# Two solves start later, unit 4's key loads get a pause, group norm's transposes go in pairs, and layer B's roundings are spread behind casts

## The chip, the core and the metric

The kernel runs on one core of a Trainium2 chip. The metric is device time in microseconds (us) of one execution. The core has five engines with a queue of instructions each: TensorE (PE, with its weight loads as PEld), VectorE (DVE), ScalarE (ACT), GpSimd (POOL) and SyncE (SP), whose queue here issues nearly all DMAs. Each engine takes its instructions strictly in order. An instruction that waits for a semaphore holds up everything behind it on its engine.

## The reference

The program is one inference step of a two-layer decoder for a prompt of 272 tokens (16 of them meta tokens) and 8 samples of one token, 280 columns in all. Layer A is RWKV-7 time mixing, layer B sliding-window attention with sinks.

```
for layer A (width D = 2048, 64 heads of 64):
    xm = x + (shifted x - x) * mu                      # six mixes
    r, k, v, z = xm[0..3] @ w_rkvz                      # four products, 2048 x 4096 each
    decay, a  = two small LoRA products
    kk = k * k_k ;  kk = kk / max(|kk| per head, 1e-12)  # the key norms
    k  = k * (1 + (a - 1) * k_a) ;  b = kk * a
    S_t = S * d - (S kk) b + v k ;   y_t = S_t r         # a scan over 272 tokens per head
    y  = group_norm(y) + (sum r k r_k) v ;  h += (y * silu(z)) @ w_out
shared k, v = rmsnorm(h) @ w_kv
for layer B:  q, z = rmsnorm(h) @ w_qz ; h += (attention(q, k, v) * silu(z)) @ w_o
final rmsnorm
```

Outputs are y for prompt and samples, the final states S, the shift rows and the two caches, all in float32.

## The kernel before, in words

**Products.** Every float32 weight matrix is multiplied in three passes of a reduced-precision type. `split` (L192) makes of a raw weight tile `raw` a rounded half `whi` (a cast on ACT, L195) and the rest `wlo` (a subtraction on DVE, L197). `mm3` (L216) then issues three products: `whi` times the rounded activations, `whi` times their rest, `wlo` times the rounded ones (L218 to L220). A weight tile of 128x512 (256 KB) is called a unit of weights here. The pools hold five of each of `raw`, `whi` and `wlo`, so that a cast can run at most some units ahead of PE.

**Pieces.** In layer A the order of PE's work is written out by hand. `products` (L709) goes through the large products (r, k, v, z, then a part of the output product `o`), and yields after each piece: six matmuls of 128x280. One product of 256 columns is 16 pieces, and one unit of weights serves two of them. `drive` (L610) counts the pieces in `self.pos` and lets the other streams add their own small PE work between them. A stream yields a number of pieces after which it is to be called again, and sometimes a condition. `mark` and `after` (L636, L639) are such conditions.

**The streams.** The 64 heads are 16 units of four heads (numbers 0 to 15 in names such as `kk4`; not the units of weights), and eight pairs of units (0 to 7).

- `prep` (L858) makes each unit ready: it loads k and r, and spreads the key norms over the partitions with two DMAs (`spread`, L560). It multiplies k by them into `kk` (L898, DVE). Behind that stand the rest of the inputs: two scans on DVE (L910), exponentials on ACT (L916 to L918), six POOL copies (L932), transposes on PE. The key norms of units 4 to 7 come out of `key_norms` (L552): a DMA from a DRAM tensor `kr`, a reciprocal root on DVE, and a DMA back.
- `scores`, `substitute` and `solve` (L984, L1053, L1089) build and invert a triangular matrix for each pair. `substitute` is a long run of small DVE instructions on `NL`, at whose end two DVE transposes give `TN` (L1081) and `TR` (L1082). From `TR` four ACT instructions make `TT` (L1085, 3.13 us). `solve` begins a fixed number of pieces after the scores. Its first PE work (L1102) reads `TN`, and then DVE, ACT and PE take turns (L1104, L1108, L1112, L1115, L1120, L1124, L1129, L1132).
- `chain` (L1155) runs the scan over time for a pair in five chunks.
- `group_norm` (L1256) normalises the chain's result Y, waits 36 pieces, transposes it on PE in four groups of three 128x128 transposes (L1275), three pieces apart, and adds each to the unit's bonus tile `vT` on DVE (L1276). Two groups share a PSUM tile of two banks, of which the pool has only one. The chains use the same pool. The unit's `yd` store follows (L1279).
- `decode` does the same for the samples on DVE.

**What sets DVE's, ACT's and SP's order.** The scheduler of the framework puts the instructions of the other engines in order, by its own estimates of time. Hand-set bounds on it are `high_priority` and `issue_after`, which keeps an instruction behind another one in this order. In `drive` most streams' work stands behind a late weight split (`self.los[-2]`, L621).

**Into layer B.** `out_a` (L1423) ends layer A. `phase_b` (L1469) computes k and v with four products of `w_kv`, eight units of weights each. Layer B's normalised inputs `bmh`, `bml` are made by `norm_mix` (L1459), 16 times: one ACT instruction (L1464) for the rounded half and one on DVE (L1465) for the rest. They are read later, by the q product.

Of the kernel before, what the change touches and what calls it, by code (L numbers as in the profile page):

```python
# [25 lines left out]
L = NM + SEQ  # L26
# [4 lines left out]
KT = D // 128  # L31
# [4 lines left out]
NU = NP // 2  # L36
GZ = 12
# [22 lines left out]
P_AN, P_MU, P_KVN, P_BN = 0, 16, 112, 128  # L60
# [49 lines left out]
class Kernel:  # L110
    def __init__(self, nc, tc, I, O):
        self.nc, self.tc, self.I, self.O = nc, tc, I, O

        self.raws, self.los = [], []

        self.wx = self.hold = None
        self.behind = []
        self.plan = []
        self.pools = {}
# [72 lines left out]
    def split(self, hi, lo, src):  # L192

        with self.tc.issue_after(self.root) if self.hold else contextlib.nullcontext():
            self.nc.scalar.copy(hi, src)  # L195
        with self.tc.issue_after(self.hold) if self.hold else contextlib.nullcontext():
            return self.nc.vector.tensor_tensor(lo, src, hi.bitcast(F32), op=ALU.subtract)  # L197

    def wunits(self, w, name, nk, col, nc_, per):

        nc = self.nc
        assert nc_ == 256 and per == 2, (nc_, per)
        for k0 in range(0, nk, per):
# [7 lines left out]
            self.raws.append(nc.sync.dma_start(raw.rearrange("p k c -> p (k c)"), w[col // 256, k0 // 2]))  # L211
            hi, lo = t("whi", F32R), t("wlo", F32R)
            self.los.append(self.split(hi, lo, raw))
            yield k0, hi, lo

    def mm3(self, ps, wh, wl, xh, xl, start, stop):  # L216
# [641 lines left out]
    def prep(self, u):  # L858
# [35 lines left out]

        kk = w("kk")
        self.spread(kk, self.kr[u // 4][4 * u % 16:4 * u % 16 + 4])
        for j in range(2):
            V.scalar_tensor_tensor(kk[:, j], kT[:, j], self.pcol(P_KK, p0 + j), kk[:, j], op0=MU, op1=MU)  # L898

# [189 lines left out]
    def solve(self, o):  # L1089
# [4 lines left out]
        ev = lambda n, *s: rp.tile([128, 512], F32, tag="ev", bufs=2, name=f"{n}{o}")[:, :s[0] * s[1]].rearrange(  # L1094
            "p (i t) -> p i t", t=s[1])

        yield 24 if o < 5 else 27
        ps = self.bank(self.pe, f"ps_so{o}")
        Q = [slice(32 * q, 32 * q + 32) for q in range(4)]
        for i in range(16):  # L1100
# [155 lines left out]
    def group_norm(self, o):  # L1256

        nc, rp = self.nc, self.rp
        V, A = nc.vector, nc.scalar
        MU, AD = ALU.mult, ALU.add  # L1260
        Y, var = self.Y, self.gvar
        y = Y.rearrange("p c j q i -> p (c j q) i")
        bc = lambda a: a.unsqueeze(2).to_broadcast((128, 24, 64))
        V.tensor_scalar(var, var, 1.0 / 64, GN_EPS, op0=MU, op1=AD)
        self.rsqrt(var, rp, "y", o)
        V.tensor_tensor(y, y, bc(var), op=MU)
        for j in range(4):
            u = 2 * o + j // 2
            b = self.U[u]['bonus']
            yield 3 if j else 36 if o < NU // 2 - 1 else 19  # L1270
            if j % 2 == 0:
                two = self.two_banks(f"ps_yt{o}_{j}")
            ps = two[:, j % 2]
            for c in range(3):
                nc.tensor.transpose(ps[:, 128 * c:128 * c + 128], Y[:, c, j].rearrange("p q i -> p (q i)"), self.ident)  # L1275
            V.scalar_tensor_tensor(b[:, j % 2, :L], ps[:, :L], self.pcol(P_GG, 4 * o + j), b[:, j % 2, :L],  # L1276
                                   op0=MU, op1=AD)
            if j % 2 and o < GZ // 2:
                nc.sync.dma_start(self.yd[u // 2][:, 2 * (u % 2):2 * (u % 2) + 2, :L], b[:, :, :L])  # L1279
        self.mark('g', o)  # L1280

# [141 lines left out]
    def out_a(self):  # L1423
# [11 lines left out]
        for k in range(KT):  # L1435
# [15 lines left out]
            if k >= KT - 2:  # L1451
                nc.tensor.matmul(pst[:, :N], ones, acc if k == KT - 2 else sq, start=k == KT - 2,
                                 stop=k == KT - 1)
        units = self.wunits(self.I['w_kv'][0], "kv", KT, 0, 256, 2)
        self.kvu = itertools.chain([next(units) for _ in range(5)], units)
        nc.scalar.activation(self.rb, pst[:, :N], AF.Ln, bias=self.epst, scale=1.0 / D)
# [12 lines left out]
    def phase_b(self):  # L1469
# [18 lines left out]
        with self.tc.tile_pool(name="kvm", bufs=2, reuse_waits="tile") as pool:  # L1488
# [44 lines left out]
            dma(f('p_cache_v')[0], self.Vd)  # L1533
            dma(f('s_cache_k')[:, WIN - 1], ksn)
            dma(O['s_cache_v'][:, WIN - 1], self.Vn[0:64:8, :, 0])
            self.bmx = [self.norm_mix(bp, "bm", P_BN, k) for k in range(KT)]
        self.wx = None
        self.close("wx0", "st0", "kv")
        right = dict(side="right", reuse_waits="tile")
# [433 lines left out]
```

## Time and profile before

| | |
|---|---|
| median of 3 runs | 2120.92 us (2119.35 to 2124.57) |
| the profiled execution | 2118.32 us |
| its span, first to last instruction | 2116.5 us |
| PE busy | 2064.9 us (98%) |
| DVE busy | 1697.8 us (80%) |
| ACT busy | 1263.8 us (60%) |
| mean granted TensorE clock | 0.99 |

The profiled execution has 1.8 us outside its span and lies 2.6 us under the median of the three runs. In timelines each row gives the start in us from the span's start, the duration, engine, line, operation, tiles, shape, count, and in brackets the engine's idle time before the row with what ended it. Matmuls overlap: a row's duration is not its spacing, which the next row's start gives. A granted clock of 0.50 means that TensorE ran at half speed in that stretch.

### The profile page before, as it was taken

The page shows a single profiled execution, that of the slowest core. Times are in us where ns is not written, and L with a number is a line of the kernel's source. Part 1 is how long each engine was busy: PE and PEld are TensorE (multiplying, and loading weights), DVE is VectorE, ACT ScalarE, POOL GpSimd, SP SyncE. Part 2 cuts the span into 40 slices and gives each one's busy share as a digit, 9 for nine tenths or more (in the row PEclk, how much of TensorE's full clock was granted, in tenths as well). Part 3 has the DMA queues.
Part 4 walks back from the last instruction along what each step waited for, and adds up shares of the span by engine and source line. Part 5 has one row for each costly group of instructions (what it writes and reads, how often), then busy time and mean ns, then how long its engine had stood idle before and what let it go on. Part 6 is the DMA issues. An engine that isn't in the chain of part 4 may idle for free.

```text
span 2116.5 us, 55871 instructions
## 1 busy us (share of the span) xinstructions
PE 2064.9 (98%) x21420; PEld 1965.8 (93%) x21420; DVE 1697.8 (80%) x4112; ACT 1263.8 (60%) x2790; POOL 122.5 (6%) x188
## 2 busy tenths in 40 slices
PE   9999999899999999999999999999999999999997
PEld 7999899889899989899999999999999999999997
DVE  8867777687678878888888788997888888878885
ACT  3457766576766757767676445565565655544443
POOL 0011100001010010100100001100000000000000
PEclk9999999999999999999999999999999999999999
DMA  7898667658756876777657687757455444567774
GB/s 258 314 312 250 189 213 241 188 181 290 216 180 205 260 229 198 211 217 222 203 152 246 207 257 243 247 172 227 132 167 156 146 155 130 181 210 247 232 219 132
DMA packets 276356, 446.28 MB, mean 211 GB/s; under 512 B 54056, under 2 KB 97768, under 8 KB 275696
## 3 DMA queue, kind: packets, MB, share of 16 engines
q1 hardware_dynamic: 275656, 441.66, 66.6%
q8 instruction: 168, 2.75, 0.5%
q10 hardware_dynamic: 432, 1.05, 0.1%
q14 instruction: 100, 0.82, 0.1%
HBM read 381.69 MB, written 65.03 MB: 211 GB/s over the span
## 4 chain that ended last, share of the span: by engine, by line
PE 87%; DVE 5%; ACT 3%; DMA 3%; issue 2%; SPq 0%; POOL 0%; DVEq 0%; POOLq 0%; ACTq 0%
PE ps_z L218 6%; PE ps_z L219 6%; PE ps_z L220 6%; PE ps_k L218 3%; PE ps_ob L218 3%; PE ps_ob L220 3%; PE ps_v L218 3%; PE ps_ob L219 3%; PE ps_r L218 3%; PE ps_q L218 3%; PE ps_q L220 3%; PE ps_q L219 3%; PE ps_k L219 3%; PE ps_k L220 3%; PE ps_v L220 3%; PE ps_v L219 3%
## 5 line engine op out<-in xcount | busy, mean ns | idle before, releaser
L218 PE MATMUL ps_z<-mhlm,whi_z 128*128 128x280 f32 x512 | 158.6, 310 | 2.8 <-ACT sr L937 2.0
L219 PE MATMUL ps_z<-mhlm,whi_z 128*128 128x280 f32 x512 | 150.6, 294 | 0.0
L220 PE MATMUL ps_z<-mhlm,wlo_z 128*128 128x280 f32 x512 | 150.3, 294 | 0.0
L218 PE MATMUL ps_q<-bmh,whi_qb 128*128 128x264 f32 x512 | 150.0, 293 | 0.1
L218 PE MATMUL ps_z<-bmh,whi_zb 128*128 128x264 f32 x512 | 147.4, 288 | 0.0
L220 PE MATMUL ps_q<-bmh,wlo_qb 128*128 128x264 f32 x512 | 145.6, 284 | 0.6 <-DVE wlo_qb L197 0.6
L219 PE MATMUL ps_q<-bml,whi_qb 128*128 128x264 f32 x512 | 145.6, 284 | 0.0
L219 PE MATMUL ps_z<-bml,whi_zb 128*128 128x264 f32 x512 | 145.5, 284 | 0.0
L220 PE MATMUL ps_z<-bmh,wlo_zb 128*128 128x264 f32 x512 | 145.4, 284 | 0.0
L218 PE MATMUL ps_ob<-ghi,whi_ob 128*128 128x264 f32 x512 | 145.3, 285 | 0.0
L220 PE MATMUL ps_ob<-ghi,wlo_ob 128*128 128x264 f32 x512 | 144.6, 284 | 0.0
L219 PE MATMUL ps_ob<-glo,whi_ob 128*128 128x264 f32 x512 | 144.6, 283 | 0.0
L195 ACT CAST whi_ob<-raw_ob 128x512 fp32r<-128x512 f32 x128 | 79.1, 620 | 96.9 <-PE ps_ob L219 77.8
L195 ACT CAST whi_oa<-raw_oa 128x512 fp32r<-128x512 f32 x128 | 79.2, 620 | 88.0 <-PE ps_oa L219 30.6
L197 DVE TENSOR_TENSOR wlo_r<-raw_r,whi_r 128x512 fp32r<-128x512 f32 x128 | 87.8, 691 | 42.6 <-ACT whi_r L195 41.3
L218 PE MATMUL ps_v<-mhlm,whi_v 128*128 128x280 f32 x384 | 119.8, 312 | 0.4 <-ACT st L790 0.4
L218 PE MATMUL ps_k<-mhlm,whi_k 128*128 128x280 f32 x384 | 119.1, 310 | 1.0 <-ACT st L790 1.0
L195 ACT CAST whi_v<-raw_v 128x512 fp32r<-128x512 f32 x128 | 79.0, 619 | 65.8 <-PE ps_v L219 37.7
L197 DVE TENSOR_TENSOR wlo_v<-raw_v,whi_v 128x512 fp32r<-128x512 f32 x128 | 87.3, 687 | 36.9 <-ACT whi_v L195 35.6
L195 ACT CAST whi_zb<-raw_zb 128x512 fp32r<-128x512 f32 x128 | 78.2, 619 | 62.9 <-PE ps_z L219 38.5
L220 PE MATMUL ps_k<-mhlm,wlo_k 128*128 128x280 f32 x384 | 112.4, 293 | 2.1 <-issue 2.1
L219 PE MATMUL ps_v<-mhlm,whi_v 128*128 128x280 f32 x384 | 112.7, 293 | 0.0
(478 smaller groups left out, 7604.1 us busy)
## 6 DMA issues: line engine op xcount, KB each, us to landing
raw_k<-a_w_rkvz SPq DMA_DIRECT2D x128, 256.0 KB
raw_v<-a_w_rkvz SPq DMA_DIRECT2D x128, 256.0 KB
raw_r<-a_w_rkvz SPq DMA_DIRECT2D x128, 256.0 KB
raw_z<-a_w_rkvz SPq DMA_DIRECT2D x128, 256.0 KB
raw_oa<-a_w_out SPq DMA_DIRECT2D x128, 256.0 KB
raw_qb<-b_w_qz SPq DMA_DIRECT2D x128, 256.0 KB
raw_zb<-b_w_qz SPq DMA_DIRECT2D x128, 256.0 KB
raw_ob<-b_w_o SPq DMA_DIRECT2D x128, 256.0 KB
```

The costliest lines, as they stand in the source:

```text
L195: self.nc.scalar.copy(hi, src)
L197: return self.nc.vector.tensor_tensor(lo, src, hi.bitcast(F32), op=ALU.subtract)
L218: mm(ps, wh, xh, start=start, stop=False)
L219: mm(ps, wh, xl, start=False, stop=False)
L220: return mm(ps, wl, xh, start=False, stop=stop)
```

## The change

Four places of the source change.

1. In `prep`, unit 4 alone: after the DMAs that spread its key norms, the stream yields 7 pieces before `kk` is made of them.
2. In `solve`, the number of pieces between the scores and the first PE work is 29 instead of 24 for pair 1, and 31 instead of 27 for pair 6. The other six keep theirs.
3. In `group_norm`, the four groups of three transposes become two of six, six pieces apart. Both DVE instructions of a unit follow the six transposes. The second store, and the mark that chains and later units wait for, then come 42 pieces after the start, where they came after 45.
4. In `phase_b`, the 16 calls of `norm_mix` for layer B each stand behind one cast of `w_kv`'s units: the first behind the eighth cast (unit of weights 7), the last behind the 23rd.

No operation of arithmetic is added or taken away, and the number of matmuls is the same.

```diff
@@ split, wunits: remember the cast
-            self.nc.scalar.copy(hi, src)
+            self.cast = self.nc.scalar.copy(hi, src)
...
             self.los.append(self.split(hi, lo, raw))
+            self.casts.append(self.cast)
@@ prep
         kk = w("kk")
         self.spread(kk, self.kr[u // 4][4 * u % 16:4 * u % 16 + 4])
+        if u == 4:
+            yield 7
         for j in range(2):
             V.scalar_tensor_tensor(kk[:, j], kT[:, j], self.pcol(P_KK, p0 + j), kk[:, j], op0=MU, op1=MU)
@@ solve
-        yield 24 if o < 5 else 27
+        yield (24, 29, 24, 24, 24, 27, 31, 27)[o]
@@ group_norm
-        for j in range(4):
-            u = 2 * o + j // 2
+        for i in range(2):
+            u = 2 * o + i
             b = self.U[u]['bonus']
-            yield 3 if j else 36 if o < NU // 2 - 1 else 19
-            if j % 2 == 0:
-                two = self.two_banks(f"ps_yt{o}_{j}")
-            ps = two[:, j % 2]
-            for c in range(3):
-                nc.tensor.transpose(ps[:, 128 * c:128 * c + 128], Y[:, c, j].rearrange("p q i -> p (q i)"), self.ident)
-            V.scalar_tensor_tensor(b[:, j % 2, :L], ps[:, :L], self.pcol(P_GG, 4 * o + j), b[:, j % 2, :L],
-                                   op0=MU, op1=AD)
-            if j % 2 and o < GZ // 2:
+            yield 6 if i else 36 if o < NU // 2 - 1 else 19
+            two = self.two_banks(f"ps_yt{o}_{i}")
+            for k in range(2):
+                for c in range(3):
+                    nc.tensor.transpose(two[:, k, 128 * c:128 * c + 128], Y[:, c, 2 * i + k].rearrange("p q i -> p (q i)"),
+                                        self.ident)
+            for k in range(2):
+                V.scalar_tensor_tensor(b[:, k, :L], two[:, k, :L], self.pcol(P_GG, 4 * o + 2 * i + k), b[:, k, :L],
+                                       op0=MU, op1=AD)
+            if o < GZ // 2:
                 nc.sync.dma_start(self.yd[u // 2][:, 2 * (u % 2):2 * (u % 2) + 2, :L], b[:, :, :L])
@@ out_a
+        self.kv0 = len(self.casts)
         units = self.wunits(self.I['w_kv'][0], "kv", KT, 0, 256, 2)
@@ phase_b
-            self.bmx = [self.norm_mix(bp, "bm", P_BN, k) for k in range(KT)]
+            self.bmx = []
+            for k in range(KT):
+                with self.tc.issue_after(self.casts[self.kv0 + 7 + k].ins):
+                    self.bmx.append(self.norm_mix(bp, "bm", P_BN, k))
```

The scheduler reacts to all of this, and from pair 1 on the order of DVE, ACT, POOL and SP differs in many places. Three of them follow. Line numbers of the changed source are 1 to 5 higher than those of the kernel before. The last number in a name is a serial number.

The first place is DVE while the key norms of unit 4 come in, before. `stmp1_14` and the row behind it on `NL1` are the last step of pair 1's substitution, `wlo_v_1280_12` is a weight split, `vT0` a bonus tile of pair 0's group norm.

```order
L197 TENSOR_TENSOR wlo_v_1280_12_5407<-raw_v_1280_12_5404,whi_v_1280_12_5406 128x512
L898 SCALAR_TENSOR_TENSOR kk4_5449<-kT4_5445,par_79,kk4_5449 128x280
L1075 TENSOR_TENSOR stmp1_14_5118<-NL1_5077 128x28
L898 SCALAR_TENSOR_TENSOR kk4_5449<-kT4_5445,par_79,kk4_5449 128x280
L910 SCALAR_TENSOR_TENSOR cl4_4871<-reset_1751,cl4_4871 128x272 x2
L904 TENSOR_TENSOR kT4_5445<-kT4_5445,km0_4_5454 128x280
L1077 TENSOR_TENSOR NL1_5077<-NL1_5077,stmp1_14_5118 128x2x14
L197 TENSOR_TENSOR wlo_v_1280_14_5425<-raw_v_1280_14_5422,whi_v_1280_14_5424 128x512
L904 TENSOR_TENSOR kT4_5445<-kT4_5445,km1_4_5457 128x280
L906 TENSOR_TENSOR ta4_4872<-ta4_4872,kk4_5449 128x560
L1081 STREAM_TRANSPOSE TN1_5123<-NL1_5077 128x512
L1082 STREAM_TRANSPOSE TR1_5124<-NL1_5077 128x512
```

The same place now:

```order
L197 TENSOR_TENSOR wlo_v_1280_12_5412<-raw_v_1280_12_5409,whi_v_1280_12_5411 128x512
L1078 TENSOR_TENSOR stmp1_14_5118<-NL1_5077 128x28
L1080 TENSOR_TENSOR NL1_5077<-NL1_5077,stmp1_14_5118 128x2x14
L1084 STREAM_TRANSPOSE TN1_5123<-NL1_5077 128x512
L1085 STREAM_TRANSPOSE TR1_5124<-NL1_5077 128x512
L197 TENSOR_TENSOR wlo_v_1280_14_5430<-raw_v_1280_14_5427,whi_v_1280_14_5429 128x512
L1280 SCALAR_TENSOR_TENSOR vT0_2043<-ps_yt0_0_5399,par_79,vT0_2043 128x272 x2
L197 TENSOR_TENSOR wlo_v_1536_0_5455<-raw_v_1536_0_5452,whi_v_1536_0_5454 128x512
L197 TENSOR_TENSOR wlo_v_1536_2_5483<-raw_v_1536_2_5480,whi_v_1536_2_5482 128x512
L197 TENSOR_TENSOR wlo_v_1536_4_5508<-raw_v_1536_4_5505,whi_v_1536_4_5507 128x512
L901 SCALAR_TENSOR_TENSOR kk4_5449<-kT4_5445,par_79,kk4_5449 128x280 x2
```

The two multiplications into `kk4` have moved from the place right behind `wlo_v_1280_12` to one behind four more weight splits, and `TN1`, `TR1` and group norm's two additions into `vT0` now stand ahead of them.

The second place is DVE where `TN5` is made, which the solve of pair 5 reads on PE. Before:

```order
L197 TENSOR_TENSOR wlo_z_768_0_14541<-raw_z_768_0_14538,whi_z_768_0_14540 128x512
L1075 TENSOR_TENSOR stmp5_14_13987<-NL5_13946 128x28
L197 TENSOR_TENSOR wlo_z_768_2_14629<-raw_z_768_2_14626,whi_z_768_2_14628 128x512
L1077 TENSOR_TENSOR NL5_13946<-NL5_13946,stmp5_14_13987 128x2x14
L1081 STREAM_TRANSPOSE TN5_13992<-NL5_13946 128x512
L1082 STREAM_TRANSPOSE TR5_13993<-NL5_13946 128x512
```

Now:

```order
L197 TENSOR_TENSOR wlo_z_512_6_14356<-raw_z_512_6_14353,whi_z_512_6_14355 128x512
L1078 TENSOR_TENSOR stmp5_14_13925<-NL5_13884 128x28
L1280 SCALAR_TENSOR_TENSOR vT9_10726<-ps_yt4_1_14291,par_79,vT9_10726 128x272 x2
L1080 TENSOR_TENSOR NL5_13884<-NL5_13884,stmp5_14_13925 128x2x14
L795 SCALAR_TENSOR_TENSOR st3_2_14313<-th2_0_14315,st3_2_14313 128x280
L1084 STREAM_TRANSPOSE TN5_13930<-NL5_13884 128x512
```

`TN5` stood behind the split of `z_768_2`, whose first matmul is piece 786 of PE's order, while the solve's first PE work (L1102) stood at piece 778: eight pieces apart. Now it stands behind `z_512_6`, first used at piece 774, with the solve at piece 772: two apart. Pair 5's own number of pieces has not changed.

The third place is ACT at the start of the `w_kv` products. Before (nine roundings `bmh0` to `bmh8` stand just ahead of these rows, behind the cast of `kv_0_12`):

```order
L1457 ACT_TABLE_LOAD
L1457 ACTIVATE rb_20527<-rb_20527 128x280
L1464 ACTIVATE bmh9_22753<-hT_20526,par_79 128x280
L1464 ACTIVATE bmh10_22757<-hT_20526,par_79 128x280
L1464 ACTIVATE bmh11_22761<-hT_20526,par_79 128x280
L1464 ACTIVATE bmh12_22765<-hT_20526,par_79 128x280
L195 CAST whi_kv_0_14_22101<-raw_kv_0_14_22099 128x512
L195 CAST whi_kv_256_0_22166<-raw_kv_256_0_22164 128x512
```

Now:

```order
L195 CAST whi_kv_0_12_22095<-raw_kv_0_12_22093 128x512
L1461 ACT_TABLE_LOAD
L1461 ACTIVATE rb_20527<-ps_sta_20528,epst_80 128x280
L1462 ACT_TABLE_LOAD
L1462 ACTIVATE rb_20527<-rb_20527 128x280
L195 CAST whi_kv_0_14_22101<-raw_kv_0_14_22099 128x512
L1469 ACTIVATE bmh0_22717<-hT_20526,par_79 128x280
L195 CAST whi_kv_256_0_22166<-raw_kv_256_0_22164 128x512
L1469 ACTIVATE bmh1_22721<-hT_20526,par_79 128x280
```

Thirteen of the 16 roundings stood ahead of the cast of `kv_0_14`. Now none does, and one follows each cast.

More of the change, by code (lines that the diff above doesn't have):

```diff
@@ L112, in __init__ @@
         self.nc, self.tc, self.I, self.O = nc, tc, I, O
-        self.raws, self.los = [], []
+        self.raws, self.los, self.casts = [], [], []
         self.wx = self.hold = None
```

## The prediction

> **What bounds the kernel now.** I read the busy shares first, then the chain of waits, then PE's waits, and at each long wait the timelines of PE and of the engine it waited for.
>
> ```profile
> PE 2064.9 (98%) x21420; PEld 1965.8 (93%) x21420; DVE 1697.8 (80%) x4112; ACT 1263.8 (60%) x2790; POOL 122.5 (6%) x188
> PE 87%; DVE 5%; ACT 3%; DMA 3%; issue 2%; SPq 0%; POOL 0%; DVEq 0%; POOLq 0%; ACTq 0%
> ...
> PE ps_yt L1275 <- DVE vT L1276: 8.0, 2, 6.9
> PE ps_so L1102 <- DVE TN L1081: 6.1, 2, 3.5
> ...
> PE ps_z L218 <- ACT sr L937: 2.0, 1, 2.0
> ...
> PE ps_kv L218 <- ACT whi_kv L195: 1.8, 1, 1.8
> ```
>
> PE is the bound: 98% busy, and 87% of the chain. No matmul is added or dropped, so the change can only win or lose PE's idle time, stretches at half clock, and the spacing of matmuls. The four waits above (total, times, longest, in us) are the ones that it touches. All sums are made against the profiled execution of 2118.3 us.
>
> **Part 1: the wait at 382 us.** Here are PE, then DVE, ACT and SP, and a window with PE's busy time, granted clock and DMA share.
>
> ```profile
> 381.96 0.90 PE L1275 MATMUL ps_yt<-consts,Y 128*128 128x128 f32 x3 [6.92 <-DVE vT L1276]
> ...
> 375.65 0.51 DVE L898 SCALAR_TENSOR_TENSOR kk<-kT,par,kk 128x280 f32<-128x280 f32 x1 [4.24 <-DMA kk<-kr]
> ...
> 379.90 1.03 DVE L1081 STREAM_TRANSPOSE TN<-NL 128x512 f32<-128x512 f32 x1
> 380.86 0.67 DVE L1082 STREAM_TRANSPOSE TR<-NL 128x512 f32<-128x512 f32 x1
> 381.45 0.46 DVE L1276 SCALAR_TENSOR_TENSOR vT<-ps_yt,par,vT 128x272 f32<-128x272 f32 x1
> ...
> 377.35 0.42 ACT L916 ACTIVATE Pp<-cl 128x256 f32<-128x256 f32 x1 [5.89 <-DVE cl L910]
> ...
> 370.33 0.58 SPq L563 DMA_DIRECT2D kk<-kr  x1
> ...
> 381.95:387.19 5.24, 5.23 (x23) 0.50 0.52 166
> ```
>
> PE waits 6.92 us in front of group norm's third group: the pool's only two-bank tile isn't free until DVE has added the earlier group to `vT`. DVE stood 4.24 us at `kk`, whose spread had been issued at 370.33 and was used at 375.65, 5.3 us later; then `kk`'s followers, a split, `TN` and `TR` went ahead of `vT`. After the wait PE ran 5.24 us at clock 0.50, which loses 2.6. Together 9.5 us.
>
> The 7 pieces put `kk4` behind four more weight splits and let `TN1`, `TR1` and both additions pass. The 29 pieces of solve 1 put its PE work at piece 326 (321 before), later than `TN1` by the same order; chain 1 starts those 5 pieces, 3.9 us, later, and nothing but its own group norm waits for it. Since group norm's mark now comes 3 pieces earlier, from about piece 400 on the streams stand within some pieces of where they stood. I take the whole **9.5** as gained. The cost is `kk4` itself, with its scans, exponentials, POOL copies and PE's transpose behind it:
>
> ```profile
> 390.06 0.32 POOL L932 COPY sm<-vT 128x16 f32<-128x16 f32 x1 [9.74 <-DMA vT<-vd]
> ...
> 400.33 0.27 PE L935 MATMUL ps_sm<-consts,sm 128*96 128x128 f32 x1
> ```
>
> POOL had these copies but the last done 9.74 us before it, and PE read them 10 us after that. So `kk4` may come some 10 us later and nothing waits; that cover pays for the pause. If it were gone, PE would wait at that transpose for the remainder. No DMA changes its place by more than a weight load or two on SP, so I cost SP at nothing: a weight tile then is late by one issue (0.58 us above), within the five tiles' lead. If that lead were used up, each such load would cost PE those 0.58 us.
>
> **Part 2: the transposes in pairs.** Four starts of transposes a pair become two, 32 become 16. What one costs is in PE's starts:
>
> ```profile
> 372.23 0.49 PE L1275 MATMUL ps_yt<-consts,Y 128*128 128x128 f32 x3
> 372.48 0.38 PE L218 MATMUL ps_v<-mhlm,whi_v 128*128 128x280 f32 x1
> 372.69 0.29 PE L219 MATMUL ps_v<-mhlm,whi_v 128*128 128x280 f32 x1
> 372.82 0.29 PE L220 MATMUL ps_v<-mhlm,wlo_v 128*128 128x280 f32 x1
> ...
> 898.81 0.55 PE L1275 MATMUL ps_yt<-consts,Y 128*128 128x128 f32 x3 [1.06 <-DVE vT L1276]
> ```
>
> The first product behind the transposes takes 0.21 us to the next start, the second 0.13. That is 0.08 us a switch and **1.3** for 16 fewer; zero would be the low bound, and twice that (in and out) the high one. The last row is the same two-bank wait in pair 4. The halves now stand 6 pieces apart, 36 matmuls by 0.13 or 4.7 us, where DVE had 3 pieces, 2.3 us. It should go: **1.1** (ends 0 and 1.1, since no half clock followed it).
>
> **Part 3: solve 5 and solve 6.** PE's first solve step waits when `TN` is late. The two waits, and the half clock behind the second:
>
> ```profile
> 256.24 0.44 PE L1102 MATMUL ps_so<-TN,Noff 32*32 32x16 f32 x31 [3.50 <-DVE TN L1081]
> ...
> 913.43 0.78 PE L1102 MATMUL ps_so<-TN,Noff 32*32 32x16 f32 x43 [2.56 <-DVE TN L1081]
> ...
> 913.40:919.67 6.27, 6.24 (x147) 0.50 0.85 276
> ```
>
> I compared, in pieces, where the split that stands ahead of `TN` on DVE is first used and where L1102 stands. Solve 0 is 7 pieces too early and solve 5 is 8, and these are just the two that wait; the others are at most 1 too early and wait for nothing. After the change solve 5 is 2 too early, solve 0 still 7, none other above zero. So solve 5's 2.56 should go with its half clock (half of 6.27, 3.1): **5.7**. For pair 6, 31 pieces let `TN6` and `TR6` come 4 pieces ahead of the solve, compared with now. It was ACT's work on `TR` (the row at 1037.05) that made its casts and copies late, and PE waited for one of them:
>
> ```profile
> 1037.05 3.13 ACT L1085 ACTIVATE TT<-TR,consts 128x320 f32<-128x320 f32 x4 [1.85 <-DVE TR L1082]
> ...
> 1048.41 0.29 PE L218 MATMUL ps_z<-mhlm,whi_z 128*128 128x280 f32 x1 [2.04 <-ACT sr L937]
> ...
> 1049.37:1052.79 3.42, 3.42 (x17) 0.50 0.55 155
> ```
>
> 2.04 and half of 3.42 make **3.7**. This is the least certain term: the copy `sr` is a small one among others on ACT, and between 0 and 3.7 I take the upper end because its cause moves.
>
> **Part 4: layer B's roundings.** PE waits for a cast of `w_kv`:
>
> ```profile
> 1389.57 0.40 PE L218 MATMUL ps_kv<-kvh,whi_kv 128*128 128x280 f32 x1 [1.77 <-ACT whi_kv L195]
> ...
> 1381.70 3.88 ACT L1464 ACTIVATE bmh<-hT,par 128x280 fp32r<-128x280 f32 x9
> 1385.60 1.28 ACT L1457 ACT_TABLE_LOAD   x1
> ...
> 1387.23 1.77 ACT L1464 ACTIVATE bmh<-hT,par 128x280 fp32r<-128x280 f32 x4
> 1388.91 1.12 ACT L195 CAST whi_kv<-raw_kv 128x512 fp32r<-128x512 f32 x2
> ...
> 1388.09 1.76 DVE L1465 SCALAR_TENSOR_TENSOR bml<-hT,par,bmh 128x280 fp32r<-128x280 f32 x4
> 1389.77 1.29 DVE L197 TENSOR_TENSOR wlo_kv<-raw_kv,whi_kv 128x512 fp32r<-128x512 f32 x2
> ...
> 1390.70:1394.12 3.42, 3.42 (x16) 0.50 0.61 220
> ```
>
> Thirteen roundings (3.88 + 1.77 = 5.65 us) leave the way of the cast at 1388.91; the table loads stay. The cast then comes near 1383.3 and PE wants it at 1387.8. From there one unit of weights takes ACT a cast (0.56) and a rounding (0.43), 1.0 us, and PE twelve matmuls, 1.5 us, so ACT keeps up; DVE has a split and a rest, 0.65 + 0.44 = 1.1 us. The last rounding stands nine units before the q product that reads it, 14 us of cover. Gain 1.77 + 1.7 = **3.5**; if the cover were gone, q would wait for what is left of them.
>
> **What it gives back.** All work between piece 326 and the start of layer B now meets in other orders. One new place can be read from the order: the third step of solve 5 (L1120) stands at piece 783 and waits for the `TN` that DVE makes (L1115) behind a split first used 7 pieces later. By solve 5's present wait, 2.56 and 1.7 of half clock, that costs between 0 and **4.3**; I take the upper end, since its lag is like that of the two solves that wait. Other small waits are scattered over the stretch:
>
> ```profile
> 390.00:1380.00 990.00, 970.65 (x12066) 0.99 0.71 220
> ```
>
> Its idle time is 990.0 − 970.65 = 19.35 us. Take away the 5.7 named above (1.06, 2.56 and 2.04) and 13.7 stay, which no row ties to the order. I let them keep their sum, and add one wait of 1.7 us with as much again of half clock, **3.4**, for the new meetings; zero and the 13.7 again are its ends.
>
> Sum: 9.5 + 1.3 + 1.1 + 5.7 + 3.7 + 3.5 = 24.8, less 4.3 + 3.4 = 7.7, so 17.1 us. The profiled execution goes from 2118.3 to 2101.2; the median of the runs lies 2.6 higher, so **2104 us**.
>
> [...] 8.9 of the sum (2.6, 3.1, 1.7 and 1.7, rounded) is clock that comes back.
>
> ```profile
> 667.08:670.49 3.41, 3.41 (x15) 0.50 0.87 295
> 862.17 0.39 PE L954 MATMUL ps_bo<-rklhi,ones 128*128 128x272 f32 x1 [2.03 <-ACT vk L854]
> 862.20:869.00 6.80, 6.80 (x53) 1.00 0.84 242
> ```
>
> Half clock lasts 3.41 or 3.42 us (or somewhat longer). It follows waits of 1.77, 2.04 and 2.56 us, but not that of 2.03 at 862.17, nor the 1.06. So whether a short wait is punished seems to be chance. [...]
>
> **The rivals.**
>
> *R1, DVE stays late in the z products.* DVE is 80% busy, and the waits at 913 and 1048 could come from its load there, not from the order. Then only parts 1, 2's switches and 4 come: 9.5 + 1.3 + 3.5 = 14.3, less 4.3, a gain of 10 and 2111 us. Against it: the lag in pieces tells exactly which solves wait. 0.15.
>
> *R2, the new order brings as many small waits as it removes.* The 13.7 us double, and four of the new ones draw half clock: 13.7 + 4 × 1.7 = 20.5 in place of the 7.7. Of 24.8 then 4.3 remain: 2118.3 − 4.3 + 2.6, between 2116 and 2117 us, no change. For it: orders of four engines change from pair 1 on. Against it: the waits removed have causes, and new ones need lags like 7 pieces, of which I found one. 0.13.
>
> *R3, slower: the pairs hold the two-bank tile too long.* Six transposes now fill the tile, and the next six (or a chain's) need it whole. Where DVE adds later than 6 pieces, 4.7 us, PE stands as at 382 us, for 9.5 with its half clock. In pair 4 the addition came at 898.26, 1.06 too late for 3 pieces, so its lag of 2.3 + 1.1 = 3.4 us is inside 4.7. Three of the eight pairs would cost 28.5 us: 2118.3 − 17.1 + 28.5 + 2.6, or 2132. It decides from three pairs on, since two (19) give 2123. 0.08.
>
> *R4, the clock doesn't come back behind short waits.* If half clock strikes anyway in 3.41-us windows, the sum loses 3.1 + 1.7 + 1.7 = 6.5: 2110.5 us. Against it: all three stretches begin within 1.2 us of a wait. 0.06. [...]
>
> That the change doesn't do what it says is excluded: the orders show all four edits.
>
> **How the numbers follow.** The forecast has 0.58, its own range 2094 (nothing given back: 2096, and a small wait less) to 2112 (twice the 7.7 given back). Beyond it lie R3 and part of R2, so the range is 2094 to 2118 and leaves out 0.18: R3's 0.08, 0.05 of R2, 0.05 below. About 0.3%, 6.4 us, can be told from no change: faster is below 2114.6, slower above 2127.3. Faster: 0.58 + 0.15 + 0.06, less 0.01 of R1 past the bound, 0.78. Same: R2 and that, 0.14. Slower: R3, 0.08.
>
> **What would show it.** In the changed kernel's profile: no DMA wait of DVE at `kk` near 375 us, and no PE wait at the `ps_yt` transposes above 0.5 us (part 1, 2); no L1102 wait of pair 5, though the 3.50 of pair 0 stays (part 3); no wait for `sr` near 1035; no `ps_kv` wait, with the roundings one by one between casts (part 4); clock 1.00 in those places; a wait at pair 5's third solve step. I am wrong if the idle time between 390 and 1380 us doesn't fall, if a `ps_yt` wait of several us shows up in another pair, or if PE waits at unit 4's transpose.

## The result: no gain, 0.2% slower

The changed kernel takes 2124.2 us (median of 22 runs) against 2119.6 us before (22 runs): ratio 1.0021, interval 1.0013 to 1.0029. The forecast was 2104, its range ended at 2118. The profiled execution after has a span of 2120.1 us, 3.6 more than before.

PE is still the bound (97% busy). Its waits between 377 us and the end of layer A, after (waited for: total, times, longest):

```profile
PE ps_ch L1208 <- ACT W L1199: 3.5, 4, 1.5
PE ps_z L221 <- issue: 3.4, 1, 3.4
PE ps_ch L1194 <- DVE X L1230: 2.9, 3, 1.6
PE ps_l L219 <- ACT ta L884: 2.8, 2, 2.1
PE ps_so L1111 <- issue: 2.6, 2, 2.3
PE ps_bk L1052 <- DVE E L1028: 2.6, 1, 2.6
...
PE ps_so L1123 <- DVE TN L1118: 1.8, 1, 1.8
```

Each wait that the change aimed at is gone: there is none at the transposes, none of pair 5 at its first solve step, no row for `sr`. Others stand in their place, most of them at PE's small work for the scan (`ps_ch`, the chains; `ps_l`, `prep`'s low-rank products; `ps_bk`, the scores). Where, tells a cut of both traces at the same product matmuls. PE alone, columns: stretch, its length, busy time and count, granted clock, DMA share, GB/s. Before:

```profile
388.90:790.88 401.98, 393.45 (x5312) 0.99 0.70 221
790.88:1153.39 362.51, 353.01 (x4412) 0.99 0.66 202
1153.39:1375.91 222.52, 221.19 (x2330) 1.00 0.78 246
1375.91:1462.54 86.63, 84.28 (x650) 0.98 0.67 203
```

After:

```profile
378.07:780.54 402.47, 393.58 (x5310) 1.00 0.70 221
780.54:1157.11 376.57, 356.60 (x4414) 0.98 0.65 195
1157.11:1379.20 222.09, 220.63 (x2326) 1.00 0.78 247
1379.20:1466.20 87.00, 82.95 (x651) 1.00 0.68 205
```

At the first cut the changed kernel is 10.8 us ahead (388.90 against 378.07; 1.7 of them it had before the change begins to act, at 358 us). The next 400 us cost the same in both. The second stretch, the last of v and all of z, takes 14.1 us longer: idle time goes from 9.5 to 20.0 us, and the clock falls from 0.99 to 0.98. The rest is about even. So part 1 was gained whole, and lost again in one stretch that begins 400 us later.

Four waits make half of the 20.0 us of idle time there. PE's timeline, after:

```profile
907.99 0.49 PE L221 MATMUL ps_z<-mhlm,wlo_z 128*128 128x280 f32 x1 [3.44 <-issue]
...
916.99 1.19 PE L1123 MATMUL ps_so<-TN,F 32*32 32x32 f32 x63 [1.81 <-DVE TN L1118]
...
941.38 0.40 PE L219 MATMUL ps_l<-lt5h,lhi 96*128 96x280 f32 x1 [2.06 <-ACT ta L884]
...
1010.61 0.69 PE L1052 MATMUL ps_bk<-consts,KB 64*128 64x64 f32 x8 [2.59 <-DVE E L1028]
```

And the windows of half clock at the four:

```profile
908.15:911.56 3.41, 3.41 (x16) 0.50 0.63 172
918.39:921.80 3.41, 3.41 (x16) 0.50 0.32 96
942.28:945.69 3.41, 3.41 (x27) 0.50 0.69 225
1010.55:1013.96 3.41, 3.35 (x21) 0.50 0.79 246
```

They wait 9.9 us and lose half of 13.6, 6.8, to the clock: 16.7 together. The waits that the change removed from this stretch (2.56, 2.04 and 1.06, with half of 6.27 and of 3.42) made 10.5. Half is an estimate by the granted clock, here and in the prediction: in both traces most starts of 128x280 products are 0.129 us apart at 1.00 and 0.233 at 0.50, a loss of 0.45. By that the two sums are 16.0 and 10.0. The rest of the 14.1 is in smaller waits.

### The profile page after: what moved, and what is told of

The parts are those of the page before. It is cut to its first block, busy times and chain, and to the rows that moved or that the text cites. A ratio compares the mean times of both kernels' runs of the same rounds, so it can differ in the third digit from the quotient of the medians.

```text
span 2120.1 us, 55867 instructions
## 1 busy us (share of the span) xinstructions
PE 2065.6 (97%) x21420; PEld 1963.8 (93%) x21420; DVE 1700.8 (80%) x4112; ACT 1263.4 (60%) x2790; POOL 119.2 (6%) x188
## 3 DMA queue, kind: packets, MB, share of 16 engines
q8 instruction: 168, 2.75, 0.5%
## 4 chain that ended last, share of the span: by engine, by line
PE 50%; DVE 2%; DMA 1%; issue 1%; ACT 1%; SPq 0%; POOLq 0%; DVEq 0%; ACTq 0%
PE ps_z L219 5%; PE ps_z L220 5%; PE ps_z L221 5%; PE ps_ob L219 3%; PE ps_ob L221 3%; PE ps_ob L220 3%; PE ps_q L219 3%; PE ps_q L220 3%; PE ps_q L221 3%; PE ps_o L219 2%; PE ps_oa L220 2%; PE ps_oa L219 2%; PE ps_oa L221 2%; PE ps_o L221 2%; PE ps_o L220 1%; PE ps_s L1714 1%
## 5 line engine op out<-in xcount | busy, mean ns | idle before, releaser
L219 PE MATMUL ps_v<-mhlm,whi_v 128*128 128x280 f32 x384 | 119.3, 311 | 1.1 <-ACT st L791 1.0
L219 PE MATMUL ps_k<-mhlm,whi_k 128*128 128x280 f32 x384 | 118.9, 310 | 0.1
L220 PE MATMUL ps_k<-mhlm,whi_k 128*128 128x280 f32 x384 | 112.6, 293 | 0.0
L197 DVE TENSOR_TENSOR wlo_ob<-raw_ob,whi_ob 128x512 fp32r<-128x512 f32 x128 | 87.3, 691 | 31.3 <-ACT whi_ob L195 29.1
```

Of the source, the lines that this page charges most:

```text
L219: mm(ps, wh, xh, start=start, stop=False)
L220: mm(ps, wh, xl, start=False, stop=False)
```

## The experiments

Differences are between medians, each against the kernel before in the same set of runs (2119.0 to 2120.4 us). Two changed kernels that are compared can come from different sets, between which the kernel before moves by up to 1.4 us. Ratios stand with their 95% intervals; they are not quotients of these medians. Diffs are against the kernel before, unless another is named.

**Each edit by itself.** `pause_only`:

```diff
+        if u == 4:
+            yield 7
...
-        yield 24 if o < 5 else 27
+        yield (24, 29, 24, 24, 24, 27, 27, 27)[o]
```

> The kernel before with only the 7 pieces in front of unit 4's kk, and 29 pieces for solve 1. Theory 'place': a wait that is removed stays removed, so the 9.5 us of the wait at 382 us and its half clock are gained, and the time is 9 to 10 us under before. Theory 'reshuffle': any new order of the other engines behind piece 330 brings as many small waits as it removed, wherever it comes from; then about 9 us are ahead at 390 us and nothing is left of them at 1150 us, and the time is within 3 us of before. Theory 'pairs': the transposes in pairs are what costs, so this kernel keeps its 9.5 us, as under 'place'.

Measured: 2111.4 us, −8.3, ratio 0.9959 (0.9947 to 0.9971). "Place" holds for this edit, somewhat under its 9 to 10. The trace is 10 us ahead at the cut in v and still 10.6 at 1153 us; at the transposes of pair 0 two waits of 0.8 and 1.3 us remain.

`pairs_only`: `group_norm` as in the change, all else as before.

> The kernel before with only group norm's transposes in two groups of six. 'Place' with the prediction's terms: 1.3 us from fewer switches and 1.1 from the wait at 899 us, so 2 us faster; the wait at 382 us stays, perhaps shorter. 'Pairs': the additions of a whole unit come at once to DVE and everything behind them in the z products is late, 8 to 14 us slower, with the loss between 790 and 1150 us. 'Reshuffle': the idle time between 790 and 1150 us, 9.5 us before, goes to 15 to 20 us, though none of it stands at the transposes.

Measured: 2137.6 us, +17.9, ratio 1.0082 (1.0070 to 1.0095), more than the bound of "pairs". PE between the cuts (before: 401.98 and 362.51 us long):

```profile
385.36:797.53 412.17, 395.75 (x5310) 0.99 0.69 215
797.53:1169.90 372.37, 355.45 (x4413) 0.98 0.66 197
```

Both stretches lose 10 us, and what waits in them is not the transposes: their only wait, 5.1 us, stands ahead of the first cut, at 381 us.

`round_only`: the roundings behind casts, all else as before.

> The kernel before with only the 16 roundings bound behind w_kv's casts. Nothing ahead of 1376 us changes its order, so the two traces can be compared piece by piece. The prediction's term: 3.5 us faster. Theory 'DVE is full': DVE worked 37.7 of the 38.2 us between 1390 and 1428 us of the kernel before, with three of the 16 rests in it; with 13 more by 0.43 it gets 5.6 us more, so PE gains the 1.77 and 1.7 and loses 4 to 5 us behind them, waiting for wlo_kv and for the rotation: 0.5 to 2 us slower.

Measured: 2121.9 us, +2.1, ratio 1.0013 (1.0001 to 1.0026). "DVE is full" holds, at the upper end of its bound. All of DVE, before:

```profile
1389.77:1428.00 38.23, 37.66 (x87) 0.96 0.56 171
```

The rests alone (L1465), before:

```profile
1391.00:1428.00 37.00, 1.32 (x3) 0.96 0.58 177
```

The rests in the changed kernel (L1470, the same in this one):

```profile
1392.00:1428.50 36.50, 6.42 (x13) 1.00 0.51 147
```

DVE had 0.6 us free in 38, and got 5.1 more. In `round_only` the cast comes in time, and PE gains 3.7 us on the kernel before up to 1394 us; between 1403 and 1414 us it loses 4.9. And q comes later out of DVE, so that another wait opens behind the stretch (`ps_s`, 2.5 us; the granted clock is 0.90 from 1434.45 to 1469.31 us):

```profile
PE ps_s L1711 <- DVE q L1697: 2.5, 1, 2.5
PE ps_kv L219 <- DVE rout_k L1696: 1.7, 1, 1.7
PE ps_kv L221 <- DVE wlo_kv L197: 1.1, 2, 0.6
```

`no_pairs`: the changed kernel with `group_norm` as before.

> The changed kernel with group norm's transposes as they were, in four groups of three. 'Pairs': the loss between 790 and 1150 us, some 14 us in the changed kernel, goes, and the time is 8 to 12 us under before. 'Reshuffle': another order, another set of small waits, 12 to 20 us of idle time between 790 and 1150 us, and a time within 5 us of before. 'Place': as 'pairs', since no other edit moved anything that PE waits for.

Measured: 2116.7 us, −3.0, ratio 0.9988 (0.9975 to 1.0001). By its time alone this is what "reshuffle" said. But the trace shows the loss in the second stretch gone (10.9 us ahead at its end), as "pairs" and "place" said; the roundings take 3.2 of it again, and 6.4 go between 1243 and 1300 us, which the runs on solve 6 below explain. So the pairs cost the changed kernel 7.5 us. But the edit "pairs" has two things in it: the transposes go by sixes, and the mark comes early.

**Pairs, or the mark?** `threes_42` has the early mark without pairs, `pairs_45` pairs without the early mark:

```diff
-            yield 3 if j else 36 if o < NU // 2 - 1 else 19
+            yield 2 if j else 36 if o < NU // 2 - 1 else 19
```

> The kernel before with group norm's four groups of three transposes 2 pieces apart instead of 3: no pairs, but its mark comes 42 pieces after the start, as it does with the pairs, where the kernel before has 45. Theory 'early mark': what waits for the mark starts 3 pieces earlier for each pair, and its work on DVE and ACT meets the other streams in a worse phase; then this kernel loses as the pairs alone did, 12 to 18 us slower. Theory 'pairs themselves' (six transposes and two additions at once, and the two-bank tile held whole): this kernel is within 3 us of before, apart from a few more of the short waits at the transposes (up to 1.1 us each). Theory 'any new order': somewhere from -5 to +10 us.

```diff
-            yield 6 if i else 36 if o < NU // 2 - 1 else 19
+            yield 6 if i else 39 if o < NU // 2 - 1 else 19
```

(The second diff is against `pairs_only`.)

> The kernel before with the pairs of transposes, started 3 pieces later (39 instead of 36), so that the mark comes after 45 pieces as in the kernel before. 'Early mark': what follows keeps its phase, the idle time between 390 and 1150 us stays near that of before (18 us), and the time is within 4 us of before, perhaps 2 us better from the waits at the transposes. 'Pairs themselves': 12 to 18 us slower, as the pairs alone. 'Any new order': from -5 to +10 us, and no nearer to before than the kernel with the pairs and 42 pieces was.

Measured: `threes_42` 2133.0 us, +12.6, ratio 1.0057 (1.0042 to 1.0072); `pairs_45` 2113.6 us, −6.9, ratio 0.9966 (0.9951 to 0.9982). Both times are as "early mark" said; `pairs_45` is even better than its bound. But `threes_42` proves little. Much of its loss is its own, since groups 2 pieces apart leave DVE less time:

```profile
PE ps_yt L1275 <- DVE vT L1276: 14.6, 7, 8.8
```

That was 8.0 us before. And its loss stands elsewhere than the changed kernel's: it is there by 650 us, and the second stretch takes no longer than before (361.83 against 362.51 us):

```profile
391.66:803.58 411.92, 396.33 (x5310) 0.99 0.69 215
803.58:1165.41 361.83, 351.00 (x4411) 1.00 0.67 203
```

`pairs_45` against `pairs_only` is the cleaner comparison: 25 us between the same pairs, 3 pieces apart. The pairs in themselves win: the wait at 382 us shrinks to 3.1 us at two splits of v.

`pairs_48` (42 in place of 39) asks if early is bad, or any shift.

> The kernel before with the pairs of transposes started 6 pieces later (42 instead of 36), so that the mark comes after 48 pieces, 3 later than in the kernel before. If an early mark costs because the work behind it is then too close to the work ahead of it, a late one costs nothing or little: 2108 to 2117 us. If it is the shift itself that costs, in either direction, since the kernel before had its numbers chosen around 45: 2122 to 2138 us.

Measured: 2118.5 us, −1.5, ratio 0.9994 (0.9982 to 1.0006): 5 us worse than at 45, and between the two expectations. Late costs too, a quarter of what early costs.

**The change with one number different.** `after_45`, against the changed kernel:

```diff
-            yield 6 if i else 36 if o < NU // 2 - 1 else 19
+            yield 6 if i else 39 if o < NU // 2 - 1 else 19
```

> The changed kernel with one number different: group norm's transposes start after 39 pieces instead of 36, so that its mark comes after 45 pieces, as in the kernel before, and the streams behind it keep the places they have in the changed kernel without pairs. 'Early mark' (what waits for the mark came 3 pieces too early, and that cost the changed kernel its gain): the idle time between 780 and 1150 us falls from 20 to about 10 us, and the time is 2110 to 2115 us, 8 to 14 us under the changed kernel. 'Pairs themselves': 2121 to 2126 us, as the changed kernel.

Measured: 2111.2 us, −8.8, ratio 0.9959 (0.9947 to 0.9971): 13.0 under the changed kernel. PE's waits in the second stretch:

```profile
PE ps_so L1105 <- DVE TN L1084: 3.7, 1, 3.7
PE ps_ch L1208 <- ACT W L1199: 1.1, 2, 0.7
PE ps_ch L1194 <- ACT X L1230: 0.7, 1, 0.7
PE ps_z L219 <- ACT st L791: 0.5, 1, 0.5
```

Solve 5's wait is back, since its `TN` is 8 pieces late again (behind a split first used at piece 786, with the solve at 778). In the changed kernel that wait went not by an edit of its own, but because the early mark had moved all of pair 5's work, `TN` by 12 pieces and the solve by 6.

**Who waits for the mark?** Between `after_45` and the changed kernel, PE's order differs in the transposes and in what `prep` leads to. `prep` goes on to load a unit's v when the mark is set, and its low-rank products, bonus and scores follow, 3 to 15 pieces earlier; behind them solves 5 to 7 and their chains come 6 pieces earlier. (Between `pairs_45` and `pairs_only`, too, it is `prep`'s work beside the transposes, by 1 to 11 pieces; there no solve and no chain moves, and the cost is larger.) `after_prep3`, against the changed kernel:

```diff
-            yield 0, self.after(0, ('g', u // 2 - 2))
+            yield 0, self.after(3, ('g', u // 2 - 2))
```

> The changed kernel with its pairs and its mark after 42 pieces, but prep, which goes on loading a unit's v when the mark is set, waits 3 pieces longer for it. No other stream moves: the chains' condition on the mark is met before they ask. So prep's pace is again that of the kernel before. If it is prep's work (its loads, DVE's and ACT's work for the next units) that came too early, the time is that of the changed kernel with 45 pieces, 2109 to 2114 us. If it is the transposes themselves standing 3 pieces earlier, it stays at 2121 to 2127 us.

Measured: 2120.1 us, +0.7, ratio 1.0005 (0.9993 to 1.0018). A miss on both sides: 4 us of 13 came back. In its order `prep`'s work was still one piece early for eight of the 16 units, so both causes were open. `after_prep4` has `after(4, ...)` in that line, and `after45_mark42` is the converse:

```diff
+            if i:
+                yield 3
+                self.mark('g', o)
-            yield 6 if i else 39 if o < NU // 2 - 1 else 19
+            yield 3 if i else 39 if o < NU // 2 - 1 else 19
...
-        self.mark('g', o)
```

(against `after_45`)

> The changed kernel, its transposes and mark where they are, but prep held for 4 pieces behind the mark. In PE's order this differs from the changed kernel with 45 pieces (2111.2 us) only in the 14 groups of transposes, which stand 3 pieces earlier; every other instruction of PE is at the same piece. 'Prep early' (prep's next units came too early): 2109 to 2114 us. 'Transposes early' (the two additions on DVE for a unit stand 3 pieces nearer to the end of group norm's work on Y, and that disturbs the others): 2118 to 2127 us. The run with 3 pieces came out between (2120.1), with prep one piece early.

> The other half: the transposes at 39 and 45 pieces, as in the changed kernel with 45, but the mark set at 42 pieces, so that prep goes on as early as in the changed kernel. PE's order differs from the changed kernel's only in the 14 groups of transposes, 3 pieces later. 'Prep early': 2120 to 2128 us, as the changed kernel. 'Transposes early': 2109 to 2114 us. If both cost, each of the two runs lies between 2114 and 2122 us.

Measured: `after_prep4` 2112.8 us, −6.2, ratio 0.9968 (0.9948 to 0.9988); `after45_mark42` 2126.7 us, +7.7, ratio 1.0034 (1.0020 to 1.0049). "Prep early" holds in both directions. Transposes 3 pieces early cost nothing that can be told (2112.8 against 2111.2); a mark that is 3 pieces early for `prep` costs 11.4 us where the transposes are early (`after_prep4` to the changed kernel) and 15.4 where they are late (`after_45` to this one). PE's waits in the second stretch of `after45_mark42`:

```profile
PE ps_ch L1208 <- ACT W L1199: 3.3, 4, 1.7
PE ps_z L220 <- issue: 3.1, 2, 1.7
PE ps_bk L1052 <- DVE E L1028: 2.2, 1, 2.2
PE ps_l L219 <- ACT ta L884: 2.1, 1, 2.1
PE ps_so L1123 <- DVE TN L1118: 1.8, 1, 1.8
```

These are the changed kernel's waits, line by line, with the transposes elsewhere: the order makes them, not chance.

**Solves.** `pause_solve5`, against `pause_only`: 33 in place of 27 for pair 5.

> The kernel with the pause alone, and 33 pieces instead of 27 in front of solve 5. Its wait for TN (3.9 us, and 3.4 of half clock, in the profile of the pause alone) should go by the lag, from 8 pieces to 2. By 'place' that is 5 to 7 us under the pause alone (2111.4). By 'any new order' what stands behind solve 5 shifts by 6 pieces and gives it back: within 3 us of it. The third step of solve 5 stands 1 piece too early, so by the lag no new wait comes there.

Measured: 2113.8 us against 2111.4 for the pause alone, ratios 0.9956 (0.9940 to 0.9973) and 0.9959: nothing gained. The wait for `TN` is gone, its 3.9 us and 3.4 of half clock with it. But all that follows solve 5 stands 6 pieces later, and from z's second half to the end of layer A the idle time grows by about as much (8.6 us where `pause_only` had 6.6 from the middle of z to about 1243 us, and 3.0 for 0.9 from there to w_kv).

`pause_pairs45_s6`, against `pause_pairs45` below: 31 in place of 27 for pair 6.

> The kernel with pause and pairs at 39 pieces (2106.5 us), and 31 pieces instead of 27 for solve 6. The prediction's term for it was 3.7 us (the wait of z's product for sr, 2.04, and 1.7 of half clock); in the profile of pause and pairs at 39 that wait isn't there any more, so there is nothing left to gain: 2105 to 2109 us. If the 4 pieces cost, through the chain and the group norm that start later, 1 to 4 us more.

Measured: 2109.2 us, ratio 0.9951 (0.9934 to 0.9967), against 0.9942 (0.9928 to 0.9957) without it. No gain, and the time doesn't tell whether it costs. The traces do. PE between the same products, without the edit and with it, and its waits there with it:

```profile
1221.51:1291.91 70.40, 69.95 (x543) 1.00 0.83 269
1217.35:1296.51 79.16, 75.12 (x606) 0.96 0.76 241
PE ps_o L218 <- DVE xr L785: 2.2, 1, 2.2
PE ps_dy L1340 <- DVE dy L1337: 1.9, 1, 1.9
```

The wait for `dy` stands in all five traces that have 31 pieces for solve 6 and the mark at 45 (this one, `no_pairs`, `after_45`, `after_prep3`, `after_prep4`). Their stretch from 1243 to 1300 us of the kernel before takes 63.3 to 65.3 us; in the other thirteen it takes 56.7 to 57.8, but for 60.6 in `pause_solve5`. So in the traces solve 6's 4 pieces cost some 6 us there where the mark is at 45. The changed kernel, with the early mark, doesn't show it.

**Better versions.** `pause_round2` is `pause_only` with this, the casts remembered as in the change:

```diff
+            for k in range(KT):
+                with self.tc.issue_after(self.casts[self.kv0 + 7 + (k - 7) // 2].ins) if k > 6 else contextlib.nullcontext():
+                    self.bmx.append(self.norm_mix(bp, "bm", P_BN, k))
```

> The kernel with the pause alone, and layer B's roundings placed otherwise: the first seven free, as before, the other nine two by two behind the casts from w_kv's eighth on. If DVE being full behind 1390 us is what took back the 3.5 us of the roundings, then rests that are done by then cost nothing: PE's wait for the cast goes (1.77, and 1.7 of half clock where there is one), no waits of over 0.6 us come at wlo_kv, rout_k and q, and the time is 1 to 4 us under that of the pause alone (2111.4). If PE's waits behind the casts come from ACT's roundings and not from DVE, they come again: 0 to 3 us above it.

Measured: 2112.3 us, ratio 0.9957 (0.9942 to 0.9972), the same as the pause alone. In the profile the stretch of `w_kv` is 0.9 us shorter; one wait of 0.8 us at `wlo_kv` is above the bound set.

`pause_pairs45` joins the pause and pairs at 39; `pause_pairs45_round2` adds the roundings of `pause_round2`.

> The pause alone together with the pairs at 39 pieces. The pause gave 8.5 us and the pairs at 39 gave 7, but both take away the same wait at 382 us (6.9 and 2.6 us); what the pairs have beside it are the waits at the transposes that the pause alone still had (0.8, 1.3, 0.8, 1.0, 1.1 and 0.9 us, 5.9 in all) and about 1.3 us of switches. 'Early mark': 3 to 7 us under the pause alone, 2104 to 2108 us. 'Any new order': within 3 us of the pause alone, or above it.

> As the kernel with pause and pairs at 39, and the roundings two by two with the first seven free. The roundings gave 0.9 us in the stretch of w_kv when they stood with the pause alone, and nothing that the timing could tell. So 0 to 2 us under the kernel with pause and pairs at 39; if they cost there, up to 2 us above it.

Measured: 2106.5 us, −13.5, ratio 0.9942 (0.9928 to 0.9957), and 2105.8 us, −14.2, ratio 0.9935 (0.9920 to 0.9951). Both beat both kernels; the roundings' share is too small to tell. In the profile of the first no wait at the transposes above 0.5 us is left.

## Why the prediction was wrong

Three steps failed. The one that took the time out of the range is a clause of part 1: "Since group norm's mark now comes 3 pieces earlier, from about piece 400 on the streams stand within some pieces of where they stood." It was priced at nothing. It costs 13.0 us (2124.2 to 2111.2 with the mark at 45), or 11.4 and 15.4 by the two runs on `prep`, which is more than the 7.7 allowed for all that the change gives back.

The second is part 3, which took a wait that goes for time that is gained. The third is part 4's cover, "DVE has a split and a rest", which left out DVE's other work in that stretch. Even with the mark at 45 the kernel takes 2111.2 and not 2104. By single runs the terms are 8.3 for the pause, 4.9 for the pairs, −2.1 for the roundings and −2.7 for solve 6 (2106.5 to 2109.2, not resolved): 8.4 in all, where `after_45` shows 8.8. Of the 21.7 us between the gain of 17.1 that was forecast and the 4.6 that were lost, part 3 has 12.1 (9.4 forecast), part 4 has 5.6, the mark 5.3 beyond the 7.7, part 1 has 1.2, and part 2 gave 2.5 more than forecast. That takes the terms as additive, which holds to 0.4 us in `after_45`.

- **Part 1 (9.5):** right. Alone it gives 8.3 us. In the changed kernel's trace DVE no longer waits at `kk`, and the cover held: there is no wait at unit 4's transpose.
- **Part 2 (1.3 + 1.1):** the sign was right, the size small: pairs with the mark where it was add 4.9 us to the pause (2111.4 to 2106.5), because the pause alone leaves 6.3 us of waits at transposes. The switches by themselves weren't resolved.
- **Part 3, solve 5 (5.7):** the wait went, but not by any edit to solve 5. The lag went from 8 pieces to 2 because the early mark pulled pair 5's work forward, and that early mark is what costs. Where solve 5 alone is moved (`pause_solve5`), its wait goes and nothing is gained. The new wait at the third step was foreseen (up to 4.3) and took 1.81 and 1.7 of half clock.
- **Part 3, solve 6 (3.7):** no row for `sr` is left in the changed kernel, but none either where solve 6 has its 27 pieces, and the 31 pieces cost time, as shown above. The row itself was misread. In `round_only`, where ACT has the same order up to there:

```profile
1047.05 0.26 ACT L938 COPY sr<-ps_sm 96x128 f32<-96x128 f32 x1
1048.49 0.39 PE L219 MATMUL ps_z<-mhlm,whi_z 128*128 128x280 f32 x1 [2.68 <-ACT th L794]
```

`sr` was done at 1047.31, and the same matmul stood until 1048.49. So `sr` was not what it waited for. In both traces PE went on 1.4 us after a packet of instructions had landed (1047.04 before, 1047.13 here), like the stops of the last section.
- **Part 4 (3.5):** the wait at the cast went, as worked out; the cover was wrong. What it left out is k's rotation and the state steps, which are in the same stretch. Alone the edit costs 2.1 us, where 3.5 were to be gained. A window of DVE's busy time would have shown 37.7 of 38.2.
- **What it gives back:** I let 13.7 us of scattered waits keep their sum since "no row ties" them to the order. The order does make them: those of the second stretch came again, line by line, in a second kernel with the mark at 42. R2 had the nearest picture (the small waits double), but blamed the new order at large, and I gave it 0.13.
- **R1** and **R3** are out: the wait at 913 us went, of the one at 1048 a stop of 0.9 is left ("issue", at 1051), and none came at the transposes. **R4** too: half clock came with the waits and left with them (in the second stretch of the changed kernel it stands behind the four waits shown above, 3.44, 1.81, 2.06 and 2.59 us, and nowhere else).
- **A sum:** the half-clock terms 2.6, 3.1, 1.7 and 1.7 make 9.1, not 8.9. Nothing else is worked out from it.

Why one piece of `prep` (0.8 us) should cost what `after_prep3` shows, 7 us against `after_prep4`, isn't settled. In the traces it falls 5.5 us behind `after_prep4` at one place, from 684 to 694 us: a chain waits twice, 1.69 and 0.69, and half clock lasts 6.83 behind it. The changed kernel has a wait of 1.59 at that place, without half clock. Why `prep`'s earlier work should make the later waits at all is known only as far as these rows go: which engine it holds up was not tested. That 45 is the best of 42, 45 and 48 is measured (pairs in the kernel before); that the numbers of the other streams had been fitted to it would explain it, and is only argued.

## What to carry to other kernels

In an order written out by hand, a mark that other streams wait for is part of the schedule: when an edit shortens the way to it, hold the mark where it was, and look at the edit apart from the shift. Before work is moved into a stretch, read the busy time of every engine there, not only of the one that it was moved for. And when waits are removed by a table of numbers, test each number by itself: of the four edits, the pause was worth having, and the pairs were with the mark held; moving solve 6 and the roundings as the change does was not.

## What the runs showed of the hardware

**PE stops in or behind the solve's tiny matmuls, and goes on 1.0 to 1.6 us after an instruction packet has landed.** The waits that the profile calls "issue" stand in the solve's second step (L1108, 128 tiny matmuls in 1.2 us), or within 3.2 us behind its first or second. In the changed kernel, the instruction packets from 895 to 915 us (count, MB, share):

```profile
q8 instruction: 3, 0.05, 1.0%
```

And PE's windows around the stop that ends at 907.99:

```profile
902.00:904.00 2.00, 2.00 (x136) 1.00 1.03 287
904.00:906.00 2.00, 0.56 (x14) 1.00 0.99 307
906.00:908.00 2.00, 0.01 (x1) 1.00 0.72 250
```

A packet of this queue is 16 KB; there are 168, 2.75 MB in all, and PE has 42,840 matmuls and weight loads. If the whole queue is PE's, that makes 64 bytes for each, an estimate. One such packet landed at 906.6, and PE went on 1.4 us later. In the 18 profiles of this case there are 47 "issue" waits over 0.7 us, and every one ends 1.0 to 1.6 us after such a packet has landed. They cost 2.6 to 7.0 us a run: of the 168 packets of a run, one to four brought such a stop. That these packets are what PE stood for is inferred from this; no run changed them. From 902 to 906 us the DMA share was 1.03 and 0.99; whether that made the packet late was not tested.

**How long a wait brings half clock.** Over the same profiles, counting PE's waits from 30 us on that began at full clock, and those with a stretch of 0.50 beginning in them or within 3.5 us behind them:

```
wait, us      0.5-1.5   1.5-2   2-3    over 3
waits           255       54     32      46
half clock       11       24     28      46
```

Waits that stand alone, with no other within 3.5 us, give the same picture: 4 of 205, 16 of 33, 24 of 28 and 45 of 45. So in this kernel it is hardly chance from 2 us on (74 of 78 waits), and a wait under 1.5 us is nearly free of it (11 of 255). From 1.5 to 3 us half clock followed 52 of 86 waits; why these and not the other 34 was not shown.
